# Seven block products in the down product of a hybrid layer: 3 of 8 pairs of k tiles, with one half folded into the gate

## The chip, the cores and the metric

One core of a Trainium2 chip runs one layer once. The metric is the device time of that run in microseconds. The engines are TensorE (PE; PEld is its weight load), VectorE (DVE), ScalarE (ACT), GpSimd (POOL) and SyncE (SP), which issues the DMAs. Each works through its own queue; semaphores order them. TensorE's granted clock has two levels, 2.4 GHz (1.0 in the profile) and 1.2 GHz (half clock).

## The reference

x has 256 tokens of 2048 columns, all in float32. What the change touches are the two feed-forward parts:

```python
def swiglu(h, w_gu, w_down):
    g, u = jnp.split(h @ w_gu, 2, axis=-1)
    return (jax.nn.silu(g) * u) @ w_down

x = x + 0.5 * swiglu(rms_norm(x, g_ffn1), w_gu1, w_down1)
x = x + hybrid_mixer(rms_norm(x, g_mix), ...)
x = x + 0.5 * swiglu(rms_norm(x, g_ffn2), w_gu2, w_down2)
```

w_gu is 2048 x 11264, w_down 5632 x 2048. The mixer between them (projections, short convolution, attention over a window, gates) is the same before and after.

## The kernel before

**Split operands.** Every float32 matrix is split into `hi` (a cast, on ScalarE) and `lo` (the rest, a subtraction on VectorE). A block product is three matmuls of 128x512: hi by hi, hi by lo, lo by hi. Weights come in pairs of k tiles, 128 rows x 2048 values (1 MB), by DMA. `Feed.take` hands TensorE the next part (1024 columns) and, before that, puts the splits of later parts into the queues of ScalarE and VectorE: three ahead, five where the part has a form and a second pool is open. It also runs one waiting step from the list `posts` (three if five or more wait); `run(pending)` runs one from a second list after a part's matmuls.

**Units.** A feed-forward part has eleven units of 512 gate and 512 up columns, in groups of 4, 4 and 3 (`UNITS`). A unit goes through 16 k tiles, as eight pairs. From the third unit on, `PLAN = "sppspspp"` says which pairs are taken with seven block products in place of eight (`s`, `seven`) and which plainly (`p`). Seven products need sums of the weight's four blocks (`u`, three operations on VectorE, `sums`), hence 3.5 splits and not 2, and sums of the activation's four blocks (`forms`). They are collected in banks p1, p5, p6 and p7 beside the banks a (tokens 0 to 127) and b (tokens 128 to 255). After the last `s` pair, `gather` brings p1, p5, p6 and p7 together (one copy on ScalarE, four additions on VectorE). After the last pair `combine` adds banks a and b (four operations on VectorE), ScalarE makes silu, and a product of gate and up gives `g`. Banks a and b have one buffer each: the next unit's products wait for combine. Its first nine matmuls go to p5, p7 and p6, the next three to b, then a.

**The first two units** of a part are plain. During the second, whose banks are borrowed from elsewhere, `h` is normalised pair by pair and its forms are made (`turn_into_forms`).

**Turning.** `g` is transposed by TensorE (`turns`, two steps of four transpositions, tile `at`) and split into `act`, the operand of the down product. This is done in the last pair of the next unit; for the first unit, in the second by way of `pending`; for the last unit of a group, two takes into the down product.

**Down.** After each group, `by_token` multiplies `act` by the group's k tiles of w_down, 512 columns at a time, three matmuls for each of two token halves; then `x_res += 0.5 * dn` from alternating banks (lines 566 to 582). Its operands are split three ahead. `Norm.finish` makes the factors for the norm from the sum of squares; before the first part that sum is made by `sums` on VectorE and `total` on TensorE, as steps of `pending`.

Of the kernel before, what the change touches and what calls it, by code (L numbers as in the profile page):

```python
# [12 lines left out]
F32 = mybir.dt.float32  # L13
# [6 lines left out]
P = 128  # L20
# [8 lines left out]
PLAIN = 2  # L29
HD = 64  # L30
# [23 lines left out]
def hybrid_layer(ctx: ExitStack, tc: tile.TileContext, a: dict, out: bass.AP):  # L54
# [150 lines left out]
    feed = Feed()  # L205

# [23 lines left out]
    def by_column(x, kts, name, *steps):  # L230
# [21 lines left out]
        def fold():  # L252
            t = work.tile([P, 2, S], F32, tag="fold", name=f"{name}_t")
            nc.scalar.copy(t, ps[:, :, S:])
            s = work.tile([P, 2, S], F32, tag="sum", name=f"{name}_s", bufs=4)
            nc.vector.tensor_tensor(s, ps[:, :, :S], t, op=ALU.add)
            box.append(s)
            steps[0](s)
# [16 lines left out]
    class Norm:  # L275
# [21 lines left out]
        def finish(self, ssq):  # L297
            v = small.tile([P, TB], F32, name="var")
            nc.vector.tensor_scalar(v, ssq, 1.0 / D, EPS, op0=ALU.mult, op1=ALU.add)
            self.rstd = rsqrt(v, [P, TB], "rs")  # L300
            self.diag = small.tile([P, TB, P], F32, name="diag", bufs=1)
# [10 lines left out]
        def turn_into_forms(self, p, pool):  # L312
# [6 lines left out]
            if PLAN[p] == "s":  # L319
                f = pool.tile([P, 3, P], F32, tag="rf", name="rf")  # L320
                a11, a21, a12, a22 = t[:, 0, :P], t[:, 0, P:], t[:, 1, :P], t[:, 1, P:]
                nc.vector.tensor_tensor(f[:, 0], a22, a21, op=ALU.subtract)
                nc.vector.tensor_tensor(a21, a11, a21, op=ALU.subtract)
                nc.vector.scalar_tensor_tensor(f[:, 1], a21, -1.0, a22, op0=ALU.mult, op1=ALU.subtract)
                nc.vector.tensor_tensor(f[:, 2], a12, f[:, 1], op=ALU.add)
# [66 lines left out]
    def add_ffn(w_gu, w_down, first=None):  # L392
        u0 = 0
        for units in UNITS:
            for u in range(u0, u0 + units):
# [4 lines left out]
                feed.add(w_gu[u], NKD * SUB, **hooks)  # L400
            for n in range(ND):
                feed.add(w_down[n, :, u0 * UKT * NCH:(u0 + units) * UKT * NCH], units * UKT * NCH)
# [14 lines left out]
    class Unit:  # L417


        def __init__(self, norm, fpool, late_pool, other=False):  # L420
            self.norm, self.fpool, self.pool, self.other = norm, fpool, late_pool, other
            self.begun = set()
            self.banks = {}

        def bank(self, name):
# [6 lines left out]
            if name in ("a0", "a1", "b0", "b1"):  # L432
                if name[0] not in self.banks:
                    self.banks[name[0]] = ps_mm.tile([P, 2, NCH], F32, tag="mm", name="gu")
# [13 lines left out]
        def act_part(self, k, t):  # L448
            return [self.norm.h[:, k, z, t * P:(t + 1) * P] for z in range(2)]

        def plain(self, hi, lo, w, col, last):
            for c in range(0, w, NCH):
                k, z = divmod((col + c) // NCH, 2)
                for t in range(TB):
                    self.product("ab"[t] + str(z), self.act_part(k, t), hi[:, c:c + NCH], lo[:, c:c + NCH], last)

        def seven(self, p, last):
            f = self.norm.forms[p]
            x = {"p5": [f[:, z, 0] for z in range(2)], "p6": [f[:, z, 1] for z in range(2)],
                 "a1": [f[:, z, 2] for z in range(2)], "p7": self.act_part(2 * p, 1),  # L460
                 "b0": self.act_part(2 * p + 1, 1), "a0": self.act_part(2 * p + 1, 0),
                 "p1": self.act_part(2 * p, 0)}
            for names in (("p5", "p7"), ("p6", "b0"), ("a0", "a1"), ("p1",)):
# [4 lines left out]
                run(pending)  # L468

        def gather(self):  # L470

            self.g = self.fpool.tile([P, TB, NCH], F32, tag="g", name="g", bufs=2)
            self.v = self.pool.tile([P, TB, NCH], F32, tag="v", name="v")
# [7 lines left out]
        def combine(self):  # L481
# [6 lines left out]
            posts.append(lambda: nc.vector.tensor_tensor(g, g, v, op=ALU.mult))  # L488

        def direct(self):  # L490
            g = self.g = self.fpool.tile([P, TB, NCH], F32, tag="g", name="g", bufs=2)

            def gate(t):
                nc.scalar.activation(
                    g[:, t], self.bank("ab"[t] + "0"), AF.Silu, scale=self.norm.rstd[:, t:t + 1]
                )

            def up(t):
                nc.vector.scalar_tensor_tensor(
                    g[:, t], self.bank("ab"[t] + "1"), self.norm.rstd[:, t:t + 1], g[:, t],  # L500
                    op0=ALU.mult, op1=ALU.mult,
# [4 lines left out]
        def turns(self, act, k, wide=False):  # L506

            def turn(j):
                if wide and j == 0:
                    self.wide = ps_mm.tile([P, 2, 2, S], F32, tag="mm", name="at")  # L510
                pt = transpose4(
                    [self.g[:, t, 2 * P * j:2 * P * (j + 1)] for t in range(TB)], "at",
                    self.wide[:, j] if wide else None,
                )
                posts.append(lambda: split(halves(act, k + 2 * j, k + 2 * j + 2), pt))

            return [lambda j=j: turn(j) for j in range(UKT // 2)]

    def ffn(norm, fpool, open_late, first=None, after=None, late=(), out_rows=None):
        late_pool = None if first else open_late()  # L520
        n_unit = 0
        for i, units in enumerate(UNITS):
            last = i == len(UNITS) - 1
            act = fpool.tile([P, max(UNITS) * UKT, 2, S], F32R, tag="act", name="act")
            turns = []
            for u in range(units):
                unit = Unit(norm, fpool, late_pool, n_unit == 1)
                if n_unit < PLAIN:
# [4 lines left out]
                    while col + w < end:  # L533
# [3 lines left out]
                        if first and n_unit == 0 and col + w == end - 2 * SUB:  # L537
                            late_pool = unit.pool = open_late()
                        if n_unit and 2 * (norm.turned + 1) * SUB <= col + w:
                            norm.turn_into_forms(norm.turned, late_pool)  # L540
                            norm.turned += 1
                    posts.extend(unit.direct())
                    if n_unit:
                        run(posts, len(posts))
                else:
                    for p in range(PAIRS):
                        if PLAN[p] == "s":
                            unit.seven(p, "s" not in PLAN[p + 1:])
                            if "s" not in PLAN[p + 1:]:
                                unit.gather()  # L550
                            continue
                        for j in range(2):
                            hi, lo, w, col = feed.take()
                            unit.plain(hi, lo, w, col, p == PAIRS - 1 and j == 1)
                            run(pending)
                            if p == PAIRS - 1 and j == 0:
                                run(turns, len(turns))
                    run(posts, len(posts))
                    unit.combine()
# [375 lines left out]
```

## Time and profile before

| | |
|---|---|
| median of 3 runs | 2095.58 us (2095.1 to 2096.97) |
| profiled execution | 2095.9 us |
| its span, first to last instruction | 2094.1 us |
| mean granted TensorE clock | 0.993 |
| TensorE busy | 2060.8 us, 98% |
| VectorE busy | 1478.0 us, 71% |
| ScalarE busy | 1017.8 us, 49% |
| DMA | 389.68 MB, mean 186 GB/s |

A profiled execution is one run; its times per instruction belong to its own span. Busy time of TensorE is modelled from pipelined matmuls, so the distance from one start to the next says more than the duration of one. Waits name the engine and the instruction that ended them.

### The profile page before, as it was taken

What the parts mean: (1) busy time and instruction counts of PE and PEld (TensorE: products, weight loads), DVE (VectorE), ACT (ScalarE), POOL (GpSimd) and SP (SyncE); (2) the same over time, 40 slices, a digit from 0 to 9 for tenths busy, and PEclk for the clock granted to TensorE, in tenths of its full rate; (3) what the DMA queues carried; (4) which work ended last, traced back from release to release, by engine and by line L of the source; (5) the groups of instructions that cost most, each with busy time, mean ns of one, the idle gap of its engine ahead of it and who ended that gap; (6) DMA issues with size and microseconds to landing.
All of it is one profiled execution on the core that took longest, in us unless ns stands there. A gap on an engine that the chain in (4) does not pass through costs nothing.

```text
span 2094.1 us, 24270 instructions
## 1 busy us (share of the span) xinstructions
PE 2060.8 (98%) x9578; PEld 1691.7 (81%) x9578; DVE 1478.0 (71%) x1625; ACT 1017.8 (49%) x1222; POOL 64.6 (3%) x55
## 2 busy tenths in 40 slices
PE   9989999999999999999999999998999999999999
PEld 7778888888888888877888888886888878888787
DVE  6878578985788655668666665658874888748874
ACT  6454445544455454445544444544543555435553
POOL 1000000000000000621000000000000000000000
PEclk9999999999999999999999999999999999999999
DMA  7545555445555455443555555553455555555554
GB/s 256 186 171 191 201 201 200 184 181 201 201 198 197 166 184 191 154 140 131 189 182 192 190 187 194 196 184 136 174 196 188 195 187 197 198 187 195 186 198 159
DMA packets 57939, 389.68 MB, mean 186 GB/s; under 512 B 6880, under 2 KB 8032, under 8 KB 11744
## 3 DMA queue, kind: packets, MB, share of 16 engines
q1 hardware_dynamic: 57680, 388.10, 51.3%
q8 instruction: 75, 1.23, 0.2%
q14 instruction: 40, 0.33, 0.0%
q10 hardware_dynamic: 144, 0.02, 0.0%
HBM read 386.00 MB, written 2.10 MB: 185 GB/s over the span
## 4 chain that ended last, share of the span: by engine, by line
PE 92%; DVE 4%; ACT 1%; POOL 1%; issue 1%; DMA 0%; SPq 0%; ACTq 0%; DVEq 0%; POOLq 0%
PE gu L444 11%; PE gu L445 11%; PE gu L443 11%; PE dn L225 8%; PE dn L224 8%; PE dn L223 8%; PE gate L245 6%; PE yo L245 3%; PE gate L247 3%; PE p L443 2%; PE p L444 2%; PE p L445 2%; PE xc L245 2%; DVE lo L100 2%; PE bg L245 2%; PE o L223 1%
## 5 line engine op out<-in xcount | busy, mean ns | idle before, releaser
L100 DVE TENSOR_TENSOR lo<-raw,hi 128x1024 fp32r<-128x1024 f32 (+1 forms) x729 | 872.0, 1208 | 526.5 <-ACT hi L99 519.4
L99 ACT CAST hi<-raw 128x1024 fp32r<-128x1024 f32 (+1 forms) x729 | 731.2, 1016 | 632.2 <-PE dn L225 236.3
L443 PE MATMUL gu<-hi,h 128*128 128x512 f32 x1084 | 430.2, 397 | 2.1 <-DVE v L486 1.7
L444 PE MATMUL gu<-lo,h 128*128 128x512 f32 x1084 | 428.7, 395 | 1.1 <-DVE lo L100 0.6
L445 PE MATMUL gu<-hi,h 128*128 128x512 f32 x1084 | 427.2, 394 | 0.0
L225 PE MATMUL dn<-hi,act 128*128 128x512 f32 x704 | 276.9, 393 | 0.0
L224 PE MATMUL dn<-lo,act 128*128 128x512 f32 x704 | 275.8, 392 | 0.0
L223 PE MATMUL dn<-hi,act 128*128 128x512 f32 x704 | 275.6, 391 | 0.0
L443 PEld LDWEIGHTS gu<-hi,h 128*128 128x128 f32 x1084 | 205.3, 189 | 52.5 <-issue 6.1
L444 PEld LDWEIGHTS gu<-lo,h 128*128 128x128 f32 x1084 | 205.1, 189 | 51.3 <-DVE lo L100 6.9
L445 PEld LDWEIGHTS gu<-hi,h 128*128 128x128 f32 x1084 | 204.7, 189 | 45.9 <-DVE h L287 0.4
L99 ACT CAST hi<-u 128x1024 fp32r<-128x1024 f32 x108 | 113.6, 1052 | 203.4 <-DVE u L169 159.2
L245 PE MATMUL gate<-h,hi 128*128 128x512 f32 x512 | 179.2, 392 | 0.0
L224 PEld LDWEIGHTS dn<-lo,act 128*128 128x128 f32 x704 | 132.3, 188 | 29.6
L223 PEld LDWEIGHTS dn<-hi,act 128*128 128x128 f32 x704 | 132.2, 188 | 28.7
L225 PEld LDWEIGHTS dn<-hi,act 128*128 128x128 f32 x704 | 132.3, 188 | 27.3
L247 PE MATMUL gate<-h,lo 128*128 128x256 f32 x480 | 134.4, 280 | 0.0
L100 DVE TENSOR_TENSOR lo<-u,hi 128x1024 fp32r<-128x1024 f32 x108 | 131.8, 1222 | 3.2 <-ACT hi L99 0.3
L245 PEld LDWEIGHTS gate<-h,hi 128*128 128x128 f32 x512 | 95.9, 187 | 20.6 <-issue 0.8
L245 PE MATMUL xc<-h,hi 128*128 128x512 f32 x256 | 93.3, 407 | 0.0
L247 PEld LDWEIGHTS gate<-h,lo 128*128 128x128 f32 x480 | 90.7, 189 | 0.7
L247 PE MATMUL xc<-h,lo 128*128 128x256 f32 x240 | 67.8, 282 | 0.0
(198 smaller groups left out, 2294.3 us busy)
## 6 DMA issues: line engine op xcount, KB each, us to landing
raw<-in_w_gu SPq DMA_DIRECT2D x172, 1024.0 KB, 4.6
raw<-in_w_down SPq DMA_DIRECT2D x88, 1024.0 KB, 4.6
raw<-in_w_mix SPq DMA_DIRECT2D x56, 1024.0 KB, 5.1
raw<-in_w_o SPq DMA_DIRECT2D x16, 1024.0 KB, 4.7
raw<-in_w_qkv SPq DMA_DIRECT2D x12, 1024.0 KB, 4.8
raw<-in_w_oc SPq DMA_DIRECT2D x8, 1024.0 KB, 4.8
raw<-in_w_oa SPq DMA_DIRECT2D x8, 1024.0 KB, 4.8
raw<-in_w_gu SPq DMA_DIRECT2D x7, 512.0 KB, 6.6
```

Source lines behind the costliest of these rows:

```text
L99: nc.scalar.copy(dst[0], src)
L100: nc.vector.tensor_tensor(dst[1], src, dst[0].bitcast(F32), op=ALU.subtract)
L223: nc.tensor.matmul(ps[t], x[:, k, 0, ts], hi[:, js], start=k == 0, stop=False)
L224: nc.tensor.matmul(ps[t], x[:, k, 0, ts], lo[:, js], start=False, stop=False)
L225: nc.tensor.matmul(ps[t], x[:, k, 1, ts], hi[:, js], start=False, stop=k == kts - 1)
L245: nc.tensor.matmul(ps[:, b], whi, both, start=k == 0, stop=last)
L247: nc.tensor.matmul(ps[:, b, :S], wlo, x[:, k, 0], start=False, stop=False)
L443: nc.tensor.matmul(ps, x[0], hi, start=name not in self.begun, stop=False)
L444: nc.tensor.matmul(ps, x[0], lo, start=False, stop=False)
L445: nc.tensor.matmul(ps, x[1], hi, start=False, stop=last)
```

## The change

- The down product runs through the same class `Unit` as gate and up, with plans `DOWN = {16: "spspsppp", 12: "spsppp"}` for groups of 16 and of 12 k tiles, 1024 output columns at a time (two column halves of 2048), so w_down is laid out anew. Its seven products end in a `gather` of its own and two additions into `x_res` through `posts`; `add` then adds banks b and a.
- `Act.put` replaces the plain split of a turned `act`: for an `s` pair it copies the transposed tile to SBUF, makes the sums (`seven_sums`) and their forms, and splits both.
- The half is folded into the product silu(gate) * up.
- The last pair of a unit is taken as two parts together, with bank b's products first. In the last two pairs the transpositions are one step earlier, both together.
- The first seven-product unit of each part takes its pairs in the order `FIRST = (1, 3, 2, 5, 4, 0, 6, 7)`, so with a plain one first; its weights are fetched in that order.
- In the first part the sum of squares is put one step earlier, with a step between it and `total`.
- The tiles `sum` and `pT` live in the mixer's pool.

The core of the diff:

```diff
+FIRST = (1, 3, 2, 5, 4, 0, 6, 7)
+DOWN = {16: "spspsppp", 12: "spsppp"}
...
+        def go(self, turns, end):
+
+            for i, p in enumerate(self.order):
+                kind = self.plan[p]
+                more = any(self.plan[q] == "s" for q in self.order[i + 1:])
+                if kind == "s":
+                    self.seven(p, not more)
+                    if not more:
+                        self.gather()
+                elif i + 1 < len(self.plan):
+                    for j in range(2):
+                        hi, lo, w, col = feed.take()
+                        self.plain(hi, lo, w, 2 * p * SUB + j * SUB, False)
+                        if not more:
+                            if j == 0:
+                                run(turns, len(turns))
+                            run(pending)
+                else:
+                    got = [feed.take() for _ in range(2)]
+                    for name in ("b0", "b1", "a0", "a1"):
+                        for j, (hi, lo, _, _) in enumerate(got):
+                            js = slice(NCH * int(name[1]), NCH * int(name[1]) + NCH)
+                            self.product(name, self.block(2 * p + j, "ab".index(name[0])), hi[:, js], lo[:, js], j == 1)
+                    run(pending)
+            run(posts, len(posts))
+            end()
...
-        def combine(self):
+        def glu(self):
...
-            posts.append(lambda: nc.vector.tensor_tensor(g, g, v, op=ALU.mult))
...
+            posts.append(
+                lambda: nc.vector.scalar_tensor_tensor(g, g, 0.5, v, op0=ALU.mult, op1=ALU.mult)
+            )
...
+            def both():
+                for j in range(UKT // 2):
+                    turn(j)
+                for j in range(UKT // 2):
+                    posts.append(lambda j=j: act.put(k // 2 + j, pts[j]))
...
+        def put(self, p, pt):
+            if self.plan[p] == "s":
+                t = feed.pool.tile([P, 2, S], F32, tag="rn", name="rn")
+                nc.scalar.copy(t, pt)
+                f = feed.pool.tile([P, 3, P], F32, tag="rf", name="rf")
+                seven_sums(f, t)
+                pt = t
+                self.forms[p] = feed.pool.tile([P, 2, 3, P], F32R, tag=f"aforms{p}", name=f"aforms{p}")
+                split((self.forms[p][:, 0], self.forms[p][:, 1]), f)
+            split(halves(self.h, 2 * p, 2 * p + 2), pt)
...
-            pending.extend([lambda: None] * 2 + turns)
-            for n in range(ND):
...
-                by_token(act, units * UKT, "dn", add, apart=n == 0 or final and n == ND - 1)
...
+            for j in range(ND // 2):
+                down = Unit(act, act.plan, fpool)
...
+                        ps = down.banks["ab"[t]].rearrange("p z n -> p (z n)")
+                        nc.vector.tensor_tensor(xs, xs, ps, op=ALU.add)
...
+                def gather(down=down, j=j):
...
+                    posts.append(lambda: nc.vector.tensor_tensor(x_res[:, :, n0], x_res[:, :, n0], g, op=ALU.add))
+                    posts.append(lambda: nc.vector.tensor_tensor(x_res[:, :, n1], x_res[:, :, n1], v, op=ALU.subtract))
+
+                down.gather = gather
+                down.go(turns if j == 0 else [], add)
...
-            pending[:0] = [skip] * 4
-            pending.extend((norm1.sums, norm1.total, lambda: None, norm1.spread))
+            pending[:0] = [skip] * 3
+            pending.extend((norm1.sums, skip, norm1.total, lambda: None, norm1.spread))
```

`seven_sums` is the four operations of `turn_into_forms` on 128x128 blocks, moved into a function.

## Rows read from the trace of the kernel before

**Rows 1.** The page, busy time, share and instructions by engine
```profile
PE 2060.8 (98%) x9578; PEld 1691.7 (81%) x9578; DVE 1478.0 (71%) x1625; ACT 1017.8 (49%) x1222; POOL 64.6 (3%) x55
```

**Rows 2.** TensorE's waits: for whom, us in total, times, longest
```profile
PE p L443 <- ACT g L494: 11.2, 2, 5.6
PE at L111 <- DVE act L100: 8.4, 2, 4.2
PE qp L111 <- POOL qall L690: 3.3, 1, 3.3
PE gu L443 <- DVE v L486: 1.7, 8, 0.2
PE ssq L363 <- DVE acc L358: 1.6, 1, 1.6
```

**Rows 3.** A stretch inside a down product: length, busy time (instructions) by engine
```profile
480.00:550.00 70.00, 70.00 (x308) 57.43 (x307) 3.85 (x6) 1.00 0.53 193
```

**Rows 4.** VectorE in time, end of a unit: start, us, instruction, [idle before]
```profile
364.47 1.22 DVE L100 TENSOR_TENSOR lo<-raw,hi 128x1024 fp32r<-128x1024 f32 x1 [0.15 <-ACT hi L99]
365.61 0.68 DVE L476 TENSOR_TENSOR g<-g,p 128x512 f32<-128x512 f32 x1
...
368.37 1.22 DVE L169 TENSOR_TENSOR u<-raw 128x1024 f32<-128x1024 f32 x1
...
370.96 2.51 DVE L100 TENSOR_TENSOR lo<-u,hi 128x1024 fp32r<-128x1024 f32 x2
373.38 1.82 DVE L100 TENSOR_TENSOR lo<-raw,hi 128x1024 fp32r<-128x1024 f32 x2
375.12 1.28 DVE L100 TENSOR_TENSOR act<-at,act 128x512 fp32r<-128x512 f32 x2
376.32 0.68 DVE L483 TENSOR_TENSOR g<-g,gu 128x512 f32<-128x512 f32 x1
...
378.11 0.68 DVE L486 TENSOR_TENSOR v<-gu,v 128x512 f32<-128x512 f32 x1
```

**Rows 5.** TensorE in time, the same end of a unit
```profile
363.65 0.40 PE L445 MATMUL p<-hi,h 128*128 128x512 f32 x1
...
372.23 1.04 PE L111 MATMUL at<-ident,g 128*128 128x128 f32 x8
...
375.61 0.39 PE L445 MATMUL gu<-hi,h 128*128 128x512 f32 x1
...
378.94 0.47 PE L443 MATMUL gu<-hi,h 128*128 128x512 f32 x1 [0.18 <-DVE v L486]
```

**Rows 6.** Stretches behind three waits; the granted clock is third from the end
```profile
42.00:47.00 5.00, 5.00 (x17) 3.99 (x17) 3.97 (x12) 1.74 (x4) 0.00 (x0) 0.66 0.58 210
112.00:118.00 6.00, 6.00 (x15) 4.70 (x16) 3.68 (x4) 2.93 (x4) 0.00 (x0) 0.52 0.18 74
376.00:384.00 8.00, 7.78 (x33) 5.75 (x33) 6.54 (x9) 4.84 (x5) 0.00 (x0) 1.00 0.35 131
```

**Rows 7.** TensorE in time, second unit's end and the first seven-product unit
```profile
105.86 0.39 PE L445 MATMUL gu<-hi,h 128*128 128x512 f32 x1
111.83 0.80 PE L443 MATMUL p<-hi,forms 128*128 128x512 f32 x1 [5.58 <-ACT g L494]
```

**Rows 8.** VectorE in time, inside the second unit
```profile
84.51 0.56 DVE L100 TENSOR_TENSOR forms<-rf,forms 128x384 fp32r<-128x384 f32 x1 [0.58 <-ACT forms L99]
...
88.21 1.23 DVE L100 TENSOR_TENSOR lo<-raw,hi 128x1024 fp32r<-128x1024 f32 x1 [1.00 <-ACT hi L99]
```

**Rows 9.** Groups by line and shape: count, busy us, mean ns, idle before
```profile
L488 DVE TENSOR_TENSOR g<-g,v 128x1024 f32<-128x1024 f32 x18 | 21.9, 1219 | 1.1 <-ACT g L487 1.1
...
L100 DVE TENSOR_TENSOR forms<-rf,forms 128x384 fp32r<-128x384 f32 x6 | 3.3, 558 | 3.5 <-ACT forms L99 3.5
...
L322 DVE TENSOR_TENSOR rf<-rn 128x128 f32<-128x128 f32 x6 | 1.8, 292 | 0.2
```

**Rows 10.** DMA issues by line: count, KB each, median us to landing
```profile
out_x<-x_res SPq DMA_DIRECT2D x8, 256.0 KB, 2.3
```

More of the change, by code (lines that the diff above doesn't have):

```diff
@@ L254, in fold @@
             nc.scalar.copy(t, ps[:, :, S:])
-            s = work.tile([P, 2, S], F32, tag="sum", name=f"{name}_s", bufs=4)
+            s = place["mix"].tile([P, 2, S], F32, tag="sum", name=f"{name}_s", bufs=4)
             nc.vector.tensor_tensor(s, ps[:, :, :S], t, op=ALU.add)
@@ L300, in finish @@
             self.rstd = rsqrt(v, [P, TB], "rs")
+            self.half = small.tile([P, TB], F32, name="half")
+            nc.vector.tensor_scalar(self.half, self.rstd, 0.5, None, op0=ALU.mult)
             self.diag = small.tile([P, TB, P], F32, name="diag", bufs=1)
@@ L523, in ffn @@
             last = i == len(UNITS) - 1
-            act = fpool.tile([P, max(UNITS) * UKT, 2, S], F32R, tag="act", name="act")
+            act = Act(fpool, units * UKT)
             turns = []
             for u in range(units):
-                unit = Unit(norm, fpool, late_pool, n_unit == 1)
+                unit = Unit(norm, PLAN, fpool, n_unit == 1, FIRST if n_unit == PLAIN else None)
                 if n_unit < PLAIN:
@@ L545, in ffn @@
                 else:
[L546 to L559, printed above, removed]
-                run(turns, len(turns))
+                    unit.go(turns, unit.glu)
                 turns = unit.turns(act, u * UKT, n_unit == 0)
@@ L567, in ffn, with add @@
                     late.pop(0)()
-            pending.extend([lambda: None] * 2 + turns)
-            for n in range(ND):
-                final = out_rows is not None and last
-                def add(ps, n=n, last=last, final=final):
-                    cols = slice(n * NCH, (n + 1) * NCH)
-                    for t in range(TB):
+            for j in range(ND // 2):
+                down = Unit(act, act.plan, fpool)
+                cols = slice(2 * j * NCH, (2 * j + 2) * NCH)
+                def add(down=down, j=j, cols=cols):
+                    for t in (1, 0):
@@ L582, in ffn @@
[L582 to L584 removed]
+                        after(2 * j)
+                        after(2 * j + 1)
+                def gather(down=down, j=j):
+                    g = fpool.tile([P, TB, NCH], F32, tag="g", name="g", bufs=2)
+                    v = feed.pool.tile([P, TB, NCH], F32, tag="v", name="v")
+                    b = down.banks
+                    n0 = slice(2 * j * NCH, (2 * j + 1) * NCH)
+                    n1 = slice((2 * j + 1) * NCH, (2 * j + 2) * NCH)
+                    nc.scalar.copy(g[:, 0], b["p1"])
+                    nc.vector.tensor_tensor(g[:, 1], g[:, 0], b["p6"], op=ALU.add)
+                    nc.vector.tensor_tensor(v[:, 0], g[:, 1], b["p5"], op=ALU.add)
+                    nc.vector.tensor_tensor(g[:, 1], g[:, 1], b["p7"], op=ALU.add)
+                    nc.vector.tensor_tensor(v[:, 1], g[:, 1], b["p5"], op=ALU.add)
+                    posts.append(lambda: nc.vector.tensor_tensor(x_res[:, :, n0], x_res[:, :, n0], g, op=ALU.add))
+                    posts.append(lambda: nc.vector.tensor_tensor(x_res[:, :, n1], x_res[:, :, n1], v, op=ALU.subtract))
```

91 lines of the change are left out of this document (52 added, 39 removed).

## The prediction, written before the changed kernel ran

> **What bounds the kernel now.** I read the table of busy time first: TensorE 98%, VectorE 71%, ScalarE 49% [rows 1]. Then TensorE's waits [rows 2]: the five longest entries come to 26 us, most of it at the start of each feed-forward part, and among them are eight waits of 0.2 us on the last subtraction of a gate/up unit (`v`). So TensorE sets the time nearly everywhere, and what a removed product is worth is its start-to-start time: 308 down products touch a 70 us stretch, so (70.0 + 0.4) / 308 = 0.229 us each [rows 3].
>
> The average of 71% hides what matters here, so I read VectorE in order of time at the end of one gate/up unit [rows 4] beside TensorE [rows 5]. There, VectorE works without a pause from the first `gather` addition (365.61) to the last subtraction (378.8): gather 2.8 us, sums `u` and their two `lo` 5.0, two more `lo` 1.7, two `act` 1.2, then the four operations on banks a and b (combine). TensorE's last matmul of the unit ends at 376.0; it covers 2 us with nine products p5, p7, p6 of the next unit, then needs bank b, then a, and is held from 378.59 to 378.94. The two engines meet here almost exactly: VectorE has no spare time between the last p1 product (ends 364.05) and the end of the unit. The busy share doesn't show that; the eight short waits do.
>
> **What the change removes.** Eight seven-product pairs per feed-forward part (3 + 3 + 2), two column halves each, one block product of three matmuls less: 8 x 2 x 3 x 2 parts = 96 matmuls, 96 x 0.229 = -22.0 us, all on TensorE's path.
>
> The sum of squares moves a step ahead of its matmul: the 1.6 us wait [rows 2] goes, and with it the spell at half clock behind it. The granted clock after that wait was 0.66 over 5 us [rows 6], which costs 0.34 x 5 = 1.7 us: -3.3 together (0 to -3.3).
>
> In the second unit both transposes of the first unit now stand together, so the 4.2 us wait for `act` in each part goes [rows 2]; and the first seven-product unit begins with a plain pair, which lies over the 5.6 us wait for `g` [rows 2, 7]. But who sets those waits? VectorE is busy with turning `h` into forms; its one idle second in the second half of that unit, at 87.2, is a wait for TensorE [rows 8]. Its queue now holds more: the forms of the first `act` pair, four operations of 0.292, a wait of 0.58 for ScalarE and 0.558 [rows 8, 9], some 2.7 us with the casts that stand between; less the idle second; plus 0.5 for two full `lo` instead of one and a half ahead of the last form. So the gate activation, and p5 behind it, comes at about 111.83 + 2.2 = 114.0 instead of 111.83, with 24 matmuls (5.5 us) done by then that were still ahead before: 3.3 us gained per part, -6.5 in all. The waits themselves stay, as waits for `lo` and `g`. Bounds: 0, and -16.7 if both 5.6 us waits and the 2.9 us at half clock behind each [rows 6] vanish.
>
> **What it adds at the end of a unit.** Each seven-product pair of the down product needs forms of `act`, made when the unit before is turned, in the last two pairs of the next unit: VectorE's full stretch. At VectorE, last pairs of the second unit of the second group of four, before:
>
> ```order
> L100 TENSOR_TENSOR lo<-u,hi 128x1024 x2
> L100 TENSOR_TENSOR lo<-raw,hi 128x1024
> L100 TENSOR_TENSOR lo<-raw,hi 128x512
> L100 TENSOR_TENSOR act<-at,act 128x2x256 x2
> L483 TENSOR_TENSOR g<-g,gu 128x512
> ```
>
> And the same place now (`rf`, `aforms`: sums and forms of the pair; L516 is the first operation of glu, which was combine):
>
> ```order
> L102 TENSOR_TENSOR lo<-u,hi 128x1024 x2
> L564 TENSOR_TENSOR rf<-rn 128x128
> L565 TENSOR_TENSOR rn<-rn 128x128
> L566 SCALAR_TENSOR_TENSOR rf<-rn 128x128
> L567 TENSOR_TENSOR rf<-rn,rf 128x128
> L102 TENSOR_TENSOR aforms_2835<-rf,aforms_2835 128x384
> L102 TENSOR_TENSOR act<-rn,act 128x2x256
> L102 TENSOR_TENSOR lo<-raw,hi 128x1024
> L102 TENSOR_TENSOR act<-at,act 128x2x256
> L102 TENSOR_TENSOR lo<-raw,hi 128x512
> L516 TENSOR_TENSOR g<-g,mm 128x512
> ```
>
> Five operations have come in ahead of the four that free the banks, and nothing has gone. They cost 4 x 0.33 start to start, then ScalarE's cast of the forms (0.58 of waiting), 0.56, and 0.3 because `lo<-raw` now waits for its own cast behind two others: 2.8 us. Combine moves from 376.32 to 379.1; bank b is free at 380.5 where TensorE wants it at 377.9 (2.6 us), bank a 0.5 after TensorE wants that. `hi` and `lo` of the next unit queue behind and come 0.3 late. That is 3.4 us per unit, where eight units lost 0.55 before (0.35 at the gap, 0.2 at the next `lo`). Seven such units per part (2 + 3 + 2), 14 in all: 14 x 3.4 - 8 x 0.55 = +43. Bounds: the five operations alone less 0.3 of slack, 14 x 1.4 - 4 = +16; with every cast a further 0.6 late, +52.
>
> A wait of 2.6 us lies above the shortest one (1.6) that half clock followed. Behind the 1.6 and the 5.6 us wait the clock fell, behind one of 0.2 us it stayed at full speed [rows 6]. I take 1.2 us per unit between 0 and 1.7: +17 (0 to 24).
>
> **What it adds in the first half of each down product.** The last unit's `act` is turned there too, but now behind the gather of the down product and its two additions into `x_res`. VectorE, first down product, before (`dn` banks; the operands of the last unit's act early, among splits):
>
> ```order
> L100 TENSOR_TENSOR lo<-raw,hi 128x1024 x3
> L100 TENSOR_TENSOR act<-at,act 128x2x256
> L100 TENSOR_TENSOR lo<-raw,hi 128x1024
> L100 TENSOR_TENSOR act<-at,act 128x2x256
> L100 TENSOR_TENSOR lo<-raw,hi 128x1024 x4
> ```
>
> And now, from the last gather addition on (`g`, `v`: what the seven products give to the two column halves):
>
> ```order
> L648 TENSOR_TENSOR v<-g,p_1587 128x512
> L102 TENSOR_TENSOR lo<-raw,hi 128x1024
> L649 TENSOR_TENSOR x_res<-x_res,g 128x2x512
> L102 TENSOR_TENSOR lo<-raw,hi 128x1024
> L650 TENSOR_TENSOR x_res<-x_res,v 128x2x512
> L171 TENSOR_TENSOR u<-raw 128x1024
> L172 TENSOR_TENSOR u<-u,raw 128x512
> L173 TENSOR_TENSOR u<-u,raw 128x512
> L102 TENSOR_TENSOR lo<-u,hi 128x1024
> L102 TENSOR_TENSOR act<-at,act 128x2x256
> L102 TENSOR_TENSOR lo<-u,hi 128x1024
> L102 TENSOR_TENSOR act<-at,act 128x2x256
> ```
>
> On ScalarE, the same place:
>
> ```order
> L644 COPY g<-p_1628 128x512
> L101 CAST hi<-raw 128x1024 x2
> L101 CAST hi<-u 128x1024
> L101 CAST act<-at 128x2x256
> L101 CAST hi<-u 128x1024
> L101 CAST act<-at 128x2x256
> ```
>
> The cast of `act` stands behind the cast of `u`, which is of the next column half and waits for VectorE's sums. Both queues run in order, and TensorE wants this `act` two parts and a transposition after the last p1 product: 24 x 0.229 + 0.8 - 0.2 = 6.1 us after it. From the gather of [rows 4]: it starts 1.6 after p1 and takes 2.8; two `lo` and two additions of 128x1024 (no row of their own; the nearest, L488, 1.22 [rows 9]) at 1.14 start to start, 4.6; the first sum 1.2: 10.1. Cast of `hi` and of `act`: 11.7. TensorE stands 5.6 us, does two matmuls, then waits until VectorE has done the rest of `u` (11.5), `lo` (12.7) and `act` (13.3). Lost: 13.3 - 6.1 - 0.5 = 6.7 us, in six places: +40 (30 if TensorE reaches the place 1.7 later than I have it; 46 with a further microsecond of casts). Behind TensorE's waiting matmul stands its whole queue; VectorE and ScalarE then wait for buffers, so nothing is won back. Half clock behind a 5.6 us wait cost 2.9 [rows 6]; I take 2.2, between that and 1.7: +13 (10 to 17).
>
> **Smaller ones.** At the end of a down column half bank a is freed 0.5 us late (two 1.2 us additions into `x_res` behind a `lo`), 10 x 0.5; the same for four unit ends without act, +2. The mixer's first input is turned later, among the first projections: +4 (0 to 8). The last output is twice as large an addition and DMA as the two that end the run now (256 KB land in 2.3 us [rows 10]): +1. Together +12 (0 to 20). DMA bytes and matmul shapes are otherwise the same.
>
> A rule speaks the other way. The Trainium skill (Trace Analysis, "Identifying the Most-Contended Engine") says the engine with the highest occupancy is the one to relieve first. By that rule TensorE at 98% gets shorter and VectorE at 71% has room; that is the first rival below. Rows 4 and 5 show VectorE full where the new work falls, so I give it little.
>
> **Sum**, from the profiled execution's span of 2094.1: -22.0 - 3.3 - 6.5 + 43 + 17 + 40 + 13 + 12 = +93, so 2187; with the 1.8 us around the span (2095.9 - 2094.1), 2189. The profiled run was 0.3 above the median, which changes nothing.
>
> **Rivals.** (1) VectorE hides it all. Bank b is now finished 12 matmuls before bank a, and splits are made up to five ahead; if VectorE reached glu within 12 us of the last p1, as it did at 376.32 (12.3), no new wait would arise. Then the old ones go as well: -22.0 - 3.3 - 2 x (4.2 + 0.2 + 1.7) - 2 x (5.6 + 2.9) + 7 of small ends, 2048 us. Against it: the order adds work to a queue with no pause in it. It decides from about 0.3 us of slack; the new work is 1.7 at the least. Chance 0.12, since orders of three engines leave much unseen. (2) The down halves hide theirs, say because the sums are done early, and only the unit ends cost: 2094.1 - 31.8 + 43 + 17 + 12 + 1.8 = 2136, chance 0.08. (3) Only the down halves cost: 2094.1 - 31.8 + 40 + 13 + 12 + 1.8 = 2129, chance 0.08. (4) Gains and losses just cancel: 0.02. My forecast, both surface: 0.70.
>
> **Range and chances.** The terms' own bounds give 2108 to 2236 for the forecast; ends of several terms together are unlikely, so 2125 to 2212, which takes in (2) and (3). About 0.2% is what a measurement of this kernel can tell from no change. Faster 0.12, within it 0.02, slower 0.86.
>
> **What would show it.** TensorE's waits in the changed kernel: six of 5 to 6 us for the cast of `act` in the first half of a down product, each followed by a shorter one for VectorE's `act`; about 14 of 2 to 3 us for `v` of glu; a granted clock well below 0.993 in the mean; 9,482 matmuls and weight loads, 96 fewer than now, each still 0.229 apart; p5 of the first seven-product unit still waiting some 6 us. If `act` and `v` hardly appear among the waits, rival (1) holds and I misjudged VectorE's room. If the wait for `act` is near 2.6 us, the sums were ready and only the cast's place costs.

## The result, and the profile after

The changed kernel takes 2182.96 us (median of 4 runs, 2181.84 to 2186.89) against 2095.34: 1.042 times as long, interval 1.040 to 1.044. The forecast was 2189. The profiled execution has a span of 2180.7, 86.6 us more than before, at a mean granted clock of 0.978 against 0.993.

Busy time by engine after, as in [rows 1]:

```profile
PE 2068.0 (95%) x9482; PEld 1686.1 (77%) x9482; DVE 1692.0 (78%) x1916; ACT 1086.1 (50%) x1330; POOL 64.4 (3%) x55
```

TensorE has the 96 matmuls fewer, and VectorE 214 us more to do. TensorE's waits after, as in [rows 2] (for whom, us in total, times, longest):

```profile
PE mm L451 <- DVE v L517: 35.4, 14, 2.5
PE mm L451 <- ACT act L101: 33.7, 6, 6.1
PE p L451 <- ACT g L530: 12.0, 2, 6.0
PE mm L451 <- DVE v L519: 5.4, 17, 0.3
PE mm L452 <- DVE lo L102: 3.9, 5, 1.8
PE qkv L226 <- DVE x_res L631: 3.3, 1, 3.3
PE qp L113 <- POOL qall L760: 3.1, 1, 3.1
PE mm L453 <- DVE act L102: 2.0, 6, 0.3
```

The first two lines are the forecast's two large terms in number and size: 14 unit ends, up to 2.5 us each, and six first halves of a down product, 5.4 to 6.1. The wait for ssq and the 4.2 us ones for act are gone; a wait for `lo` of 1.8 and one for `x_res` of 3.3 are new.

VectorE in time at a unit end of the second group, to be read against [rows 4]:

```profile
377.50 0.68 DVE L509 TENSOR_TENSOR g<-g,p 128x512 f32<-128x512 f32 x1
...
380.26 1.22 DVE L171 TENSOR_TENSOR u<-raw 128x1024 f32<-128x1024 f32 x1
...
382.85 2.51 DVE L102 TENSOR_TENSOR lo<-u,hi 128x1024 fp32r<-128x1024 f32 x2
385.28 0.28 DVE L564 TENSOR_TENSOR rf<-rn 128x128 f32<-128x128 f32 x1
...
387.12 0.56 DVE L102 TENSOR_TENSOR aforms<-rf,aforms 128x384 fp32r<-128x384 f32 x1 [0.58 <-ACT aforms L101]
387.64 0.69 DVE L102 TENSOR_TENSOR act<-rn,act 128x512 fp32r<-128x512 f32 x1
388.60 1.23 DVE L102 TENSOR_TENSOR lo<-raw,hi 128x1024 fp32r<-128x1024 f32 x1 [0.26 <-ACT hi L101]
...
390.94 0.68 DVE L516 TENSOR_TENSOR g<-g,mm 128x512 f32<-128x512 f32 x1
391.54 0.68 DVE L517 TENSOR_TENSOR v<-mm,v 128x512 f32<-128x512 f32 x1
```

From the first gather addition to the first operation on the banks it takes 13.4 us (377.50 to 390.94), where it took 10.7 (365.61 to 376.32): 2.7 more, of which the five new operations and their wait are 385.28 to 387.64. TensorE there, as in [rows 5]:

```profile
389.34 0.39 PE L453 MATMUL p<-hi,forms 128*128 128x512 f32 x1
392.27 0.50 PE L451 MATMUL mm<-hi,h 128*128 128x512 f32 x1 [2.55 <-DVE v L517]
...
393.56 0.47 PE L451 MATMUL mm<-hi,h 128*128 128x512 f32 x1 [0.32 <-DVE v L519]
```

The nine products of p5, p7 and p6 are done at 389.7, and TensorE goes on, with bank b, 2.55 us later. In the first half of a down product ScalarE, and then TensorE, show the other wait:

```profile
236.53 1.05 ACT L101 CAST hi<-raw 128x1024 fp32r<-128x1024 f32 x1 [0.41 <-PE mm L453]
243.99 1.04 ACT L101 CAST hi<-u 128x1024 fp32r<-128x1024 f32 x1 [6.41 <-DVE u L171]
244.94 0.58 ACT L101 CAST act<-at 128x512 fp32r<-128x512 f32 x1
```

```profile
236.33 1.04 PE L113 MATMUL at<-ident,g 128*128 128x128 f32 x8
...
239.74 0.39 PE L453 MATMUL mm<-hi,act 128*128 128x512 f32 x1
245.57 0.79 PE L451 MATMUL mm<-hi,act 128*128 128x512 f32 x1 [5.44 <-ACT act L101]
...
247.12 0.80 PE L453 MATMUL mm<-hi,act 128*128 128x512 f32 x1 [0.33 <-DVE act L102]
```

ScalarE idles 6.4 us for VectorE's sum `u` while the tile `at`, transposed by 237.4, stands behind it in the queue. What the clock does behind the new waits, to be read against [rows 6] (the granted clock is third from the end):

```profile
392.00:398.00 6.00, 5.41 (x16) 4.01 (x17) 4.54 (x6) 4.83 (x5) 0.00 (x0) 0.72 0.51 175
...
439.68:445.68 6.00, 5.60 (x22) 4.06 (x23) 4.53 (x5) 4.85 (x5) 0.00 (x0) 1.00 0.42 164
...
245.57:253.57 8.00, 7.67 (x23) 5.70 (x24) 2.53 (x3) 1.54 (x2) 0.00 (x0) 0.68 0.01 5
...
42.00:47.00 5.00, 4.40 (x14) 3.52 (x14) 4.96 (x8) 2.27 (x3) 0.00 (x0) 0.66 0.63 211
```

The first row is 0.28 x 6 = 1.7 us lost behind a unit end. Ten of the fourteen unit ends lose that much; the other four lose nothing, as the second row shows for an equal wait: 1.2 in the mean, as forecast. The third is 0.32 x 8 = 2.6 behind an act wait, counted from its end; the six lose 2.2 to 3.3, 2.6 in the mean (forecast 2.2). Over the span, 0.022 x 2181 - 0.007 x 2094 = 33 us more go to the clock.

By stage, from the first matmul of each to the first of the next (the wait at the end of a group's last unit falls into its down product):

| us | before | after | forecast of the difference |
|---|---|---|---|
| first group's gate/up, both parts | 388.6 | 389.4 | 8.6 of two unit ends, less 9.8 |
| other gate/up, four stages | 605.0 | 625.0 | 26 of six unit ends |
| down products of 16, four | 355.2 | 392.2 | 36 (53/6 + 4.3 - 4.1 each) |
| down products of 12, two | 140.5 | 166.4 | 21; 6 more at the half ends of all six and at the last output |
| mixer | 599.8 | 602.8 | 4 |

### The profile page after: what moved, and what is told of

It reads as the page before. It is cut to its first block, busy times and chain, and to the rows that moved or that the text cites. A ratio compares the mean times of both kernels' runs of the same rounds, so it can differ in the third digit from the quotient of the medians.

```text
span 2180.7 us, 24485 instructions
## 1 busy us (share of the span) xinstructions
PE 2068.0 (95%) x9482; PEld 1686.1 (77%) x9482; DVE 1692.0 (78%) x1916; ACT 1086.1 (50%) x1330; POOL 64.4 (3%) x55
## 4 chain that ended last, share of the span: by engine, by line
PE 72%; DVE 18%; ACT 5%; issue 3%; POOL 1%; DMA 0%; SPq 0%; ACTq 0%; DVEq 0%; POOLq 0%
PE mm L453 13%; PE mm L451 12%; PE mm L452 12%; DVE lo L102 7%; PE gate L248 5%; ACT hi L101 4%; PE yo L248 3%; PE gate L250 3%; PE p L451 3%; PE p L452 3%; PE p L453 3%; PE xc L248 2%; PE bg L248 1%; PE o L228 1%; PE o L226 1%
## 5 line engine op out<-in xcount | busy, mean ns | idle before, releaser
L451 PE MATMUL mm<-hi,h 128*128 128x512 f32 x956 | 380.2, 398 | 26.8 <-DVE v L517 20.2
L452 PE MATMUL mm<-lo,h 128*128 128x512 f32 x956 | 376.2, 393 | 4.2 <-DVE lo L102 3.9
L453 PE MATMUL mm<-hi,h 128*128 128x512 f32 x956 | 375.5, 393 | 0.0
L451 PE MATMUL mm<-hi,act 128*128 128x512 f32 x512 | 209.6, 409 | 51.6 <-ACT act L101 33.7
L451 PEld LDWEIGHTS mm<-hi,h 128*128 128x128 f32 x956 | 181.5, 190 | 77.8 <-DVE v L517 25.2
L102 DVE TENSOR_TENSOR lo<-u,hi 128x1024 fp32r<-128x1024 f32 x172 | 210.2, 1222 | 37.6 <-ACT hi L101 32.7
L452 PEld LDWEIGHTS mm<-lo,h 128*128 128x128 f32 x956 | 181.2, 190 | 44.3 <-DVE lo L102 8.4
L453 PEld LDWEIGHTS mm<-hi,h 128*128 128x128 f32 x956 | 181.0, 189 | 38.5 <-DVE h L290 0.4
L453 PE MATMUL mm<-hi,act 128*128 128x512 f32 x512 | 206.7, 404 | 2.0 <-DVE act L102 2.0
L452 PE MATMUL mm<-lo,act 128*128 128x512 f32 x512 | 205.3, 401 | 0.1
L451 PEld LDWEIGHTS mm<-hi,act 128*128 128x128 f32 x512 | 99.8, 195 | 83.3 <-ACT act L101 36.2
L453 PEld LDWEIGHTS mm<-hi,act 128*128 128x128 f32 x512 | 99.2, 194 | 28.7 <-DVE act L102 7.6
L452 PEld LDWEIGHTS mm<-lo,act 128*128 128x128 f32 x512 | 100.0, 195 | 20.9 <-DVE lo L102 1.0
L171 DVE TENSOR_TENSOR u<-raw 128x1024 f32<-128x1024 f32 x86 | 104.8, 1219 | 0.0
```

What stands on the lines that cost most here:

```text
L102: nc.vector.tensor_tensor(dst[1], src, dst[0].bitcast(F32), op=ALU.subtract)
L171: nc.vector.tensor_tensor(u[:, :2], b[:, 0:4:3], b[:, 1:2].broadcast_to([P, 2, NCH]), op=ALU.add)
L451: nc.tensor.matmul(ps, x[0], hi, start=name not in self.begun, stop=False)
L452: nc.tensor.matmul(ps, x[0], lo, start=False, stop=False)
L453: nc.tensor.matmul(ps, x[1], hi, start=False, stop=last)
```

## The experiments

The reason on record was one of place: VectorE has work put ahead of what frees the banks, and ScalarE's cast of act stands behind that of `u`. The rival that the runs had to test is one of amount: VectorE has no time for the new work wherever it is put. All ratios are to the kernel before. A table at the end of this section has the runs by stage.

**The forms of act behind glu.**

```diff
 def put(self, p, pt, hold):
     if self.plan[p] == "s":
         nc.scalar.copy(t, pt)
+        def rest():                 # sums, forms and act of the pair
...
+        held.append(rest)
...
     run(posts, len(posts))
     end()
+    posts.extend(held)
```

> The sums and splits of the seven-product act pair are issued after glu instead of before it; the same work, 14 times, a few operations later in VectorE's queue. Theory (place, not amount): the 14 waits for v of glu in the changed kernel (35.4 + 5.4 us) and the half clock behind them (20 us) vanish: 2183 - 61 = 2122 us, between 2115 and 2130; the six waits for act stay at 33.7 us. Rival (VectorE is simply too full): the same work comes back as waits of TensorE for lo or forms in the first pairs of the next unit, and the time stays above 2150.

Measured 2174.64, ratio 1.038 (1.036 to 1.040). TensorE's waits:

```profile
PE p L451 <- ACT hi L101: 11.9, 6, 2.0
PE mm L452 <- DVE lo L102: 11.4, 14, 1.8
PE mm L451 <- DVE v L521: 5.7, 18, 0.3
PE p L452 <- DVE lo L102: 5.4, 6, 1.0
```

The 35.4 us for the first v went, and some 24 came back as waits for `hi` and `lo` (11.9, 5.4, and 11.4 where it was 3.9). They stand in the third pair of the next unit or down product, not in the first as I wrote: VectorE is late with the next sums `u` there. 8 us of the 61 were gained, and the time is where the rival had it: the gate/up stages became 18 us shorter, the down products and the mixer 11 longer.

**Act first in the down product.**

```diff
-    posts.append(lambda j=j: act.put(k // 2 + j, pts[j]))
+    act.put(k // 2 + j, pts[j])     # in the down product: at once
...
     run(turns, len(turns))
+    posts.extend(self.adds)         # the additions into x_res
```

> In the first half of each down product the two act of the last unit are cast and split as soon as they are transposed, ahead of the two additions into x_res and of the sums u of the next column half. Theory (place in both queues): the six waits for the cast of act (33.7 us), the six for act behind them and most of the 23 us at half clock go; a wait under 1.5 us may stay: 2121 to 2132 us. Rival (the amount): u and lo of the next column half come later by what act takes now, and TensorE waits there: above 2150. The 14 waits for v of glu stay at 35 us in both.

2133.45, ratio 1.018 (1.016 to 1.019), 1.5 us above the theory's range. No wait for act is left among TensorE's, and the 14 for v are as before (35.4 us). This term was one of place.

**Only the additions behind act.**

```diff
-    posts.append(lambda: nc.vector.tensor_tensor(x_res[:, :, n0], ...))
+    down.adds.append(lambda: nc.vector.tensor_tensor(x_res[:, :, n0], ...))
...
     run(turns, len(turns))
+    posts.extend(self.adds)
```

> In the first half of each down product only the two additions into x_res are put behind act; the casts of act stay behind the cast of u on ScalarE. Theory (two causes in a row: VectorE's 2.3 us of additions, then the cast's place behind that of u): the six waits for act fall from 5.6 to about 3.3 us, and 6 x 2.3 us with a few us of half clock go: 2183 - 14 - 3 = 2166, between 2158 and 2172. Rival (the cast's place alone sets it): unchanged, above 2177. Rival (the additions alone): as the run with act first, 2133.

2133.14, 1.018 (1.016 to 1.019), the number of the additions alone. But it does not show that: with two steps fewer in `posts` act came a take earlier, and its first cast stood ahead of that of `u` on ScalarE. Both causes were taken away, so the run separates nothing.

**The additions moved, the casts' order kept.**

```diff
-    posts.append(lambda: nc.vector.tensor_tensor(x_res[:, :, n0], ...))
+    posts.extend([lambda: None] * 2)
...
     end()
+    posts.extend(self.adds)
```

> Four of the six first halves of a down product (not the last group of either part): the two additions into x_res move from before act into the next column half, and the order of the casts on ScalarE stays as in the changed kernel, act behind u. Theory (two causes in a row): there the wait for act falls from 5.6 to 3.3 us, the place of the cast alone still costs 3.3; at the other two places it stays at 6.1: 2183 - 4 x 2.3 - 3 of half clock = 2171, between 2164 and 2177. Rival (additions alone): the four waits vanish, 2183 - 4 x 9 = 2147. Rival (the cast's place alone): unchanged, 2180 or more.

2180.73, 1.040 (1.038 to 1.041). The waits are what the two causes in a row ask for: four of 3.2 us and two of 6.0, in one line

```profile
PE mm L451 <- ACT act L101: 24.8, 6, 6.1
```

so the additions are 2.3 us of such a wait and the cast's place 3.2. The time gained is 2 us, not 12. The four down products are 5.8 us shorter together: the clock behind the four shorter waits lost no less in the mean (below), the wait for VectorE's act behind each grew from 0.3 to as much as 0.8, and there are seven small waits for `lo` at seven-product pairs (1.6 us in all) where there were two. The mixer, which the edit leaves alone, was 2.9 us longer in the profiled execution.

**Both moves.** The edits of the first two runs together.

> Both moves together. Theory: the two terms add up, 2183 - 61 - 57 = 2065, between 2055 and 2078, faster than the kernel before (2095) by 1 to 2%. Rival (VectorE near its limit): each move lives on time that the other term's stalls gave to VectorE; with both gone new waits appear and the time is 2090 or more.

2121.59, 1.013 (1.011 to 1.014). The gains of the two runs (8 and 50) nearly add up to this one's 61, so neither move lived on the other's stalls; the time is the rival's because the first move alone had gained so little. The kernel stays slower than before.

**The forms in the second pair.**

```diff
     for i, p in enumerate(self.order):
+        if i == 1:
+            posts.extend(held)
```

> As e3, but the sums and splits of the act pair are issued behind the first pair of the next unit (or of the down product), beside plain pairs, where TensorE takes 5.5 us a pair and VectorE 2.4. Theory (VectorE has the time, but only beside plain pairs, since a seven-product pair takes it longer than TensorE): the waits of e3 in the first pair (12 for p, 10 for lo, 6 for lo behind p: 27 us) and most of the half clock behind them go: 2121.6 - 27 - 15 = 2080, between 2065 and 2092, a little faster than before. Rival (amount): the waits only move on again, to lo or hi in the next seven-product pair: above 2105.

2115.55, 1.009 (1.007 to 1.010), the rival's time again. The long waits went; new ones are

```profile
PE p L451 <- ACT aforms L101: 9.2, 2, 4.6
...
PE p L451 <- ACT hi L101: 4.0, 4, 1.0
PE p L452 <- DVE lo L102: 3.7, 16, 0.3
```

The first is one of place (in groups of 12 the forms now come just before the pair that needs them). So are the four of 1 us for `hi` in the down products of 16: on ScalarE the cast of the forms waits for VectorE's sums, and the casts of `hi` stand behind it, as `act` stood behind `u`.

```profile
479.02 0.51 ACT L101 CAST aforms<-rf 128x384 fp32r<-128x384 f32 x1 [2.66 <-DVE rf L575]
```

The rest are small waits for `lo`. By stage the moves had worked better than the whole time suggests: the other gate/up stages take 607.7 us (625.0 in the changed kernel, 605.0 before), the down products of 16 take 359.5 (392.2).

**Without the four sums.**

```diff
-    f = feed.pool.tile([P, 3, P], F32, tag="rf", name="rf")
-    seven_sums(f, t)
+    f = t.rearrange("p a (b n) -> p (a b) n", n=P)[:, :3]
```

> The changed kernel without the four sums of each act pair (seven_sums left out; the forms are cast from the transposed tile itself, so the seven products' values are others); the cast, the subtraction and every matmul stay. Theory (each operation ahead of glu is paid start to start): 14 x 4 x 0.33 = 18 us less waiting for v of glu (35 to 17), and some of the half clock behind it, 8 us: 2157, between 2150 and 2166. Rival (the wait is ScalarE's cast of the forms, not VectorE's operations): 2175 or more.

2145.71, 1.023 (1.021 to 1.025). The wait for v fell from 35.4 to

```profile
PE mm L451 <- DVE v L517: 8.1, 14, 0.6
```

which is 1.9 us for each unit end and not 1.3. The rival is excluded, but the other 0.6 us is ScalarE's: with the sums gone its cast of the forms no longer comes late, and VectorE's subtraction, which stood behind a wait of 0.58 at 387.12, follows at once.

```profile
377.22 0.55 DVE L102 TENSOR_TENSOR aforms<-rn,aforms 128x384 fp32r<-128x384 f32 x1
```

The clock gives back another 10 us (2183 - 2146 - 27).

**The down product without weight sums.** The edit is on the run with the forms in the second pair.

```diff
-    for form in "ud":
+    for form in "xx" if bare else "ud":
```

> As the run with the forms in the second pair (2115.5), but the down product's seven products take the weight's blocks themselves in place of their sums u (other values): VectorE has 6 x 2.5 = 15 us less to do in each down product of 16, 10 in each of 12, everything else in its place. Theory (amount: VectorE needs 83 us in a down product that TensorE could do in 85): the small waits and the half clock behind them go, down to 2115.5 - 6 x 8 = 2068, between 2052 and 2080. Rival (place: single waits such as that for aforms in the groups of 12): 2100 or more.

2095.52, 0.999 (0.998 to 1.000): 20 us less than with the sums, where amount said 47 and place some 15 at most, so the time lies between the two. The rows below are the second group's down product before, in the changed kernel, after all moves, and in this run:

```profile
463.40:552.20 88.80, 88.80 (x394) 72.90 (x393) 50.67 (x49) 37.00 (x37) 0.00 (x0) 1.00 0.49 178
```

```profile
481.10:578.70 97.60, 89.08 (x376) 71.14 (x375) 82.93 (x87) 47.15 (x53) 0.00 (x0) 0.95 0.48 173
```

```profile
463.40:554.00 90.60, 88.03 (x376) 70.05 (x374) 82.64 (x89) 46.11 (x52) 0.00 (x0) 0.98 0.53 186
```

```profile
461.20:547.30 86.10, 85.34 (x375) 69.04 (x374) 70.12 (x74) 46.06 (x52) 0.00 (x0) 1.00 0.56 196
```

(The columns are length, then busy us and instructions of PE, PEld, DVE, ACT and POOL.) The down product's 366 matmuls need 366 x 0.229 = 83.8 us and its eight transposes 0.9: 84.7. With 70 us of VectorE's work it takes 86.1; with 82.9 it took 97.6, and 89.1 to 90.6 after all moves. Before, VectorE had 51 of 89 us to do there. So the forecast of 8 us for each down product was more than the moves had left: the six gave 23.2 together, 3 to 5 each, and the rest of the span took 3.8 back. Nor is it shown that this is amount alone. The run takes VectorE's time away and, with the sums, a step that `hi` and `lo` of those pairs wait for; it does not separate the two.

**The new down product, plain.**

```diff
-DOWN = {16: "spspsppp", 12: "spsppp"}
+DOWN = {16: "pppppppp", 12: "pppppp"}
...
-    if j == 0:
+    if j == 0 and (i or "s" in self.plan):
         run(turns, len(turns))
```

> The changed kernel with the down product wholly plain: no sums of act, no gather, 96 matmuls more; the transposes of the last unit come after the second pair's first part. All other edits stay. Theory: what the seven products cost goes with them (2183 + 22 - 61 - 60 - 4 of small ends = 2080, between 2075 and 2095), so the other edits by themselves are worth 0 to -15 us against 2095. Rival: the other edits (both transposes together, the order of the last pair, the layout of the down product) carry part of the loss: above 2100.

2142.86, 1.022 (1.020 to 1.024): the rival's time, but not for its reason. Its two longest waits are

```profile
PE mm L451 <- DVE x_res L631: 18.4, 10, 2.9
PE mm L451 <- DVE v L517: 18.0, 6, 3.0
```

A plain down product begins with banks b and a, which have one buffer, and waits at each of its twelve openings for the last owner's additions, 2.9 to 3.0 us. In the changed kernel nine products into p5, p7 and p6 lie over that, and the waits for `x_res` there were 0.2 us. So this run has a cost that the changed kernel hides, and cannot tell the other edits' worth.

**The old down product with the other edits.**

```diff
-    down = Unit(act, act.plan, fpool)
...
+    by_token(act.h, units * UKT, "dn", add, apart=n == 0 or final and n == ND - 1)
```

> The gate/up part and the start of the changed kernel, with the down product of the kernel before (by_token, alternating banks, its layout), no forms of act: all the edits but the down product's. Theory: they are worth a few us: from the two traces the first group's gate/up takes, without its unit end, 3 us less in the first part and 6 less in the second, so 2095 - 9 = 2086, between 2080 and 2092. Rival (the plain-down run's 2143 came from these edits and not from its down product's banks): above 2110.

2074.92, 0.990 (0.989 to 0.992): faster than both, and better than expected. By stage, the first group's gate/up takes 190.2 and 184.1 us where it took 196.5 and 192.2; the rest is 0.4 to 1 us a stage, but for the first down product, which is 0.6 longer. Its longest waits:

```profile
PE p L449 <- ACT g L528: 11.4, 2, 5.7
PE mm L449 <- DVE v L517: 3.9, 12, 0.3
```

So the edits beside the down product are worth 21 us together (which of them is not separated), the reason that the rival gave for the plain-down run is excluded, and the down product by seven costs 2183 - 2075 = 108.

**One seven-product pair, then turned a pair later.**

```diff
+DOWN = {16: "sppppppp", 12: "sppppp"}       # on the changed kernel, with forms of act in the second pair
```

```diff
-    if j == 0:
+    if j == 0 and i > 1:
         run(turns, len(turns))
```

> One seven-product pair per down product instead of two or three (the first pair), its act forms issued in the second pair of the next unit: 32 matmuls fewer than without, 7.3 us. VectorE then has some 60 us of work in the 87 us of a down product of 16, where the changed kernel has 83. Theory (amount: the down product's seven products fail because they fill VectorE): no waits over 1 us inside the down products, time 2075 - 7 + 4 = 2072, between 2064 and 2082, about level with the run that keeps the old down product (2075). Rival (what comes with the down product as a unit, its banks and turning, costs by itself): 2090 or more.

> The run with one seven-product pair per down product (2106.6), with the last unit transposed one pair later (5.5 us), since its six waits for g (1.9 us each, with 1 to 5 us of half clock behind each) came from transposing before g was multiplied. Theory: both go, 2106.6 - 11.4 - 20 = 2075, between 2066 and 2084, level with the run that keeps the old down product (2075): the 32 matmuls saved (7 us) are paid back at the unit ends and at the start. Rival (the waits for g hide a later one, for act or for lo): above 2092.

2106.64, 1.005 (1.004 to 1.006), then 2091.02, 0.997 (0.997 to 0.998): the rival's time, then one between the theory's range and the rival. The first had a wait of its own:

```profile
PE at L113 <- DVE g L653: 11.4, 6, 1.9
```

Its cause is not the one in the expectation. The product that makes `g` is long done when the second transposition waits until 475.43:

```profile
470.15 1.22 DVE L525 SCALAR_TENSOR_TENSOR g<-g,v 128x1024 f32<-128x1024 f32 x1
```

Line 653 is the first addition of the down product's own gather, which reads bank p6; the tile `at` shares two buffers with p1 and p6 and has to wait until that addition has read its own. The second run has this wait no more, and no wait above 1 us in any down product, though VectorE is at 63 of 88.5 us there:

```profile
461.90:550.40 88.50, 87.91 (x387) 71.37 (x386) 63.34 (x64) 39.27 (x42) 0.00 (x0) 1.00 0.55 190
```

With 36 matmuls fewer (not 32, as I wrote) it is still 16 us slower than the run before it here. Three of the four down products of 16 take 0.6 us more than there (88.5 against 87.9) with six matmuls less: its two openings lose 1.1 and 0.7 us in gaps of up to 0.5 us around the change of banks, where the three matmuls saved in a column half are 0.7. The first group's gate/up is 4.6 and 3.0 us longer, in the unit where VectorE also turns `h`; the other gate/up stages are 4.9 longer together and the mixer 2.4.

**By stage.** The profiled executions, from first matmul to first matmul as in the table above:

| us | before | changed | forms in the second pair | no weight sums | one pair, turned later | old down product |
|---|---|---|---|---|---|---|
| first group's gate/up, both parts | 388.6 | 389.4 | 382.1 | 382.9 | 381.9 | 374.3 |
| other gate/up, four stages | 605.0 | 625.0 | 607.7 | 607.8 | 606.9 | 602.0 |
| down products of 16, four | 355.2 | 392.2 | 359.5 | 344.6 | 354.1 | 353.2 |
| down products of 12, two | 140.5 | 166.4 | 155.2 | 146.8 | 140.5 | 139.6 |
| mixer | 599.8 | 602.8 | 604.4 | 607.2 | 601.2 | 598.8 |

## Why the prediction was right, and where it was not

- **The time.** 2189 against 2183, of a sum of +93 against +86.6. That it came so near is in part luck: two misses nearly cancel. The other edits alone gave 21.2 us of span (2094.1 to 2072.9 with the old down product), where the sum has 9.8; the new down product added 107.8 to that, where the rest of the sum has 103. The terms' bounds add up to 2110 and 2233, not 2108 and 2236; nothing hangs on that.
- **Removed matmuls**, -22: the count is 96 fewer, each still 0.229 apart at full clock.
- **Sum of squares**, -3.3: the step failed. The wait for it went, and at the same place TensorE waits 1.8 us for `lo`, with the clock at 0.66 from 42 to 47 as before. With a step between the two the sum was no longer late; VectorE's next split was. Whether the one made the other late is not shown.

```profile
42.60 0.80 PE L452 MATMUL mm<-lo,h 128*128 128x512 f32 x1 [1.76 <-DVE lo L102]
...
117.07 0.80 PE L451 MATMUL p<-hi,forms 128*128 128x512 f32 x1 [5.97 <-ACT g L530]
```

- **First seven-product unit**, -6.5: p5 starts at 117.07, where I had 114.0. Against 111.83 [rows 7] that eats nearly all of the 5.5 us of matmuls already done. But 3.4 of these 5.2 us are lost in the first unit, most of them at a wait for `h` at 10.09 (0.4 us before, 1.2 now, with half clock behind it), which the sum does not have. In the second part p5 is 1.2 us later, better than the 2.2 of the forecast, and, counted from the first matmul of the part, 2.7 us later than in the run with the old down product, which makes no forms of act: that is their price in the sum. By stage, less two unit ends at the 3.3 us of the next point, the first groups gained 6 us in all against 9.8 with the point above.
- **Unit ends**, +43 and +17 of half clock: number, place and wait as forecast (2.55 us for b and 0.32 for a, against 2.6 and 0.5), and so was the clock, 1.2 in the mean. The six that can be read alone cost 20.0 / 6 = 3.3 us each against the kernel before and 23.0 / 6 = 3.8 against the run with the old down product, which has the other edits too; the forecast was 4.3.
- **Down products**, +40 and +13: the first wait as forecast (5.6 in the mean); the second is 0.3 where the sum asks for 1.1, so that the waits are 36 us and not 40. The clock was mis-sized the other way, 2.6 us behind each and not 2.2, some 16 in all. The additions' 2.3 us and the cast's place, 3.2, were measured apart.
- **Smaller ones**, +12: `x_res` at half ends 2.0 us in ten waits, the mixer 3.0, and the wait of 3.3 before qkv, which I had not named.
- **The first rival** (VectorE hides it) decided from 0.3 us of slack; there was none. The second and third would each have left out one of the first two lines of waits.

The mechanism, new work put in places where others wait for it, was right for the larger part. Moves alone, with all the work kept, took 67 of the 108 us that the down product by seven costs (2183 to 2115.5): by stage, 33 of the 39 us in the down products of 16 and 17 of the 23 in the other gate/up. My expectations of the runs that moved the forms were still too good by 36 to 57 us, since at each new place the forms stood ahead of something else.

What the account does not have is the amount. VectorE's 71% over the span [rows 1] was 51 of 89 us in a down product; the change makes it 83 where TensorE needs 85. Without the weight sums the down products are 23 us shorter, which is the most that amount can claim there. Even then the kernel is 21 us behind the run with the old down product, although it has 96 matmuls fewer: the down products of 16 win 8.6 us, and the mixer loses 8.4, the first groups 8.6, the other gate/up 5.8 and the down products of 12, with two waits of 1.9 for their forms, 7.2. Why beyond those waits is open.

## What to carry to other kernels

A product saved on the bound engine is paid for in sums on another, so set that engine's busy time against the bound engine's in the stage that changes, not over the span: at 83 us of work where the bound engine needs 85, none of the orders tried here won. Move an operation only after asking what the queue needs next at its new place; here that was a pair with sums of its own. When a change bundles several edits, run the others alone: the small ones here were worth 21 us that the large one hid.

## What the runs showed of the hardware

What a wait costs in clock is not in step with its length, nor the same each time. Behind the 14 waits of 0.6 us (without the four sums) the granted clock stayed at 1.00. Behind the 14 of 2.5 us in the changed kernel it fell ten times, to 0.72 over 6 us, and four times stayed at 1.00, though these stand at the same line of the kernel and are as long. Behind the six of 5.4 to 6.1 us it was 0.59 to 0.73 over 8 us. Behind the four of 3.2 us (the additions moved) it was 0.57 twice and 0.79 twice. First one of 0.6 us, then two of 3.2, in rows as above:

```profile
382.00:388.00 6.00, 5.38 (x21) 3.83 (x22) 4.53 (x6) 4.85 (x5) 0.00 (x0) 1.00 0.49 171
```

```profile
244.69:252.69 8.00, 7.18 (x18) 5.34 (x19) 2.15 (x3) 1.53 (x2) 0.00 (x0) 0.57 0.16 68
...
1629.39:1637.39 8.00, 7.18 (x23) 5.44 (x24) 2.63 (x3) 1.53 (x2) 0.00 (x0) 0.79 0.16 67
```

So shortening the four waits from 5.4 to 3.2 us gave nothing back in the mean (2.6 us lost behind each, in both kernels), and shortening 14 from 2.5 to 0.6 gave back every spell there was.
